# Turning attention probabilities on VectorE in 32x32 blocks, in place of identity products on TensorE

## The chip, the cores and the metric

The kernel runs on one core of a Trainium2 chip, as one launch. The metric is the time of that launch on the device in microseconds. TensorE (PE in the profile, with its weight loads as PEld) does matrix products into PSUM; VectorE (DVE), ScalarE (ACT) and GpSimd (POOL) work on the other data; SyncE (SP) issues nearly all DMA transfers. Each engine works through its own instructions in the order in which they stand; semaphores make it wait for the others.

## What is computed

A two-layer encoder trunk on 256 tokens of width 1024, in float32. Cut to what bears on the change:

```python
for layer in range(2):
    xn = rmsnorm(h)
    u, q, k, v, g_pool, g_attn = split(xn @ w_in)        # 12 heads of 128: 3 groups of 4
    pool_out = (centred means of u, minus u) @ w_pool * pool_scale
    for g, (window, dilation) in enumerate(((128, 1), (512, 4), (2048, 16))):
        logits = q_g . k_g * scale + rel_bias[bucket(offset)]   # only offsets inside the window
        o_g, lse_g = softmax(logits) @ v_g, logsumexp(logits)
    attn = sum over g of softmax(lse)_g * o_g             # one softmax over all three groups' keys
    h = h + (sigmoid(g_pool) * (pool_out @ w_a) + sigmoid(g_attn) * (attn @ w_b)) @ w_o
    xn = rmsnorm(h)
    a, gval = split(xn @ w_up)
    h = h + (gelu(conv3(a) + conv_b) * gval) @ w_down
out = rmsnorm(h)
```

## The kernel before

**Number format.** Most products are made in three: each float32 matrix is split into a high part in the faster 32-bit format of TensorE (`F32R`) and a low part, what is left. ACT casts the high part and VectorE subtracts it to get the low one. For weights these are lines 177 and 178 (`wh`, `wl`). `two_sums` (lines 482 and 484) makes one projection: eight products of 128x512 with `wh`, against the high and the low part of the activations side by side, and eight of 128x256 with `wl`.

**Weights.** The class `Weights` lists every load and every piece in the order of use. Loads go to three raw buffers through SP's queue; five buffers hold split pieces, and `get` splits three pieces ahead of the one asked for, more where buffers are free. So ACT's and VectorE's work for a product is done up to five products before TensorE comes to it.

**Order.** The layers are written out in Python. A scheduler puts each engine's instructions in order, from the program's order and its own costs; the first stage alone is scheduled by hand. Two tokens share a partition: token 2m+t is row m of half t, so a head's 256 queries are two halves of 128.

**Around the attention.** After the pooling mixer, loop `m` goes over six weight blocks of queries and keys, four projections each; then eight projections make `pa` from the pooled branch. The attention is a list `steps` that `step()` takes from between projections, so that TensorE has other work while a head's softmax is made. For each head `hh` of four (it stands for one head of each group):

- `scores` (line 866): for each half `t`, products into one PSUM tile of 128 queries x 512 keys (256 of the near group and 128 of each dilated one); VectorE adds the bias (line 881) and takes the row maximum (886), ACT takes the exponential and the sum (889), VectorE scales by the reciprocal (891, 892).
- `turn` (line 897): keys must come to the partitions for the next product. TensorE multiplies eight blocks of 128x128 with an identity (904); ACT and VectorE bring them from PSUM to a high part `pth`, a low part `ptl` and a plain `pt`.
- `weigh` (line 915): six products of `F32R` parts and plain float32 products (921, 925) into one PSUM tile, which ACT and VectorE split into `at2` (930, 931).

Steps are taken at `m >= 3` behind every second projection, and behind six of the eight of `pa`.

**Bias table.** `load_bias` and `build_bias` (lines 354 to 392) make, once, a table of bias by query and key. A one-hot matrix of 33 rows picks the bucket of every offset, and row 33 holds the mask's large negative number. Five pairs of products, with a left side of 33x4 (high part, low part), one pair for each of five kinds of block, stand between projections of the pooling mixer. The result goes to DRAM (`fd`), is written there 128 times (`sk`) and read back with shifted addresses into `bt`.

Of the kernel before, what the change touches and what calls it, by code (L numbers as in the profile page):

```python
# [10 lines left out]
F32 = mybir.dt.float32  # L11
F32R = mybir.dt.float32r
# [4 lines left out]
P = 128  # L17
# [5 lines left out]
HPG = 4  # L23
NG = 3
NH = HPG * NG
# [8 lines left out]
NT = 5  # L34
# [5 lines left out]
ENTRY = 4  # L40
# [164 lines left out]
def encoder(ctx, tc, x, w_in, w_pool, pool_scale, w_a, w_b, w_o, norm1, norm2, w_up, conv_w,  # L205
            conv_b, w_down, rel_bias, norm_f, onehot, edges, out):
    nc = tc.nc
    const = ctx.enter_context(tc.tile_pool(name="const", bufs=1))
    wpool = ctx.enter_context(tc.tile_pool(name="weights", bufs=1))
    big = ctx.enter_context(tc.tile_pool(name="big", bufs=1))  # L210
    sm = ctx.enter_context(tc.tile_pool(name="small", bufs=2))
    acc = ctx.enter_context(tc.tile_pool(name="acc", bufs=4, space=bass.MemoryType.PSUM))
# [72 lines left out]
    h = const.tile([P, 2, D], F32, name="h")  # L285
# [7 lines left out]
    ident = const.tile([P, P], F32, name="ident")  # L293
# [58 lines left out]
    bt = const.tile([P, HPG, NT * P], F32, name="bt")  # L352

    def load_bias():
        oh = big.tile([33, NT * 256], F32, tag="ybig", name="onehot_sb")
        nc.sync.dma_start(out=oh, in_=onehot)
        rb = sm.tile([33, NH], F32, tag="rb", bufs=1, name="rb")
        nc.vector.memset(rb, 1.0)
        nc.sync.dma_start(out=rb[0:32, :], in_=rel_bias)
        rh = sm.tile([33, NH], F32R, tag="ms", name="rh")  # L360
        rl = sm.tile([33, NH], F32R, tag="ms", name="rl")
        nc.vector.tensor_copy(rh, rb)
        nc.vector.tensor_sub(out=rl, in0=rb, in1=rh.bitcast(F32))
        ohr = big.tile([33, NT * 256], F32R, tag="m2", name="onehot_r")
        nc.scalar.copy(out=ohr, in_=oh)
        return rh, rl, ohr

    def build_bias(rh, rl, ohr):

        fsb = big.tile([HPG, NT * 256], F32, tag="q1", name="fsb")  # L370
        for n, g in enumerate((0, 0, 0, 1, 2)):
            ps = acc.tile([P, 512], F32, tag="acc", name="f_ps")
            for j, r in enumerate((rh, rl)):
                nc.tensor.matmul(
                    ps[:HPG, :256], r[:, g * HPG : (g + 1) * HPG], ohr[:, n * 256 : (n + 1) * 256],
                    start=(j == 0), stop=(j == 1),
                )
            nc.vector.tensor_copy(fsb[:, n * 256 : (n + 1) * 256], ps[:HPG, :256])
            yield

        n = HPG * NT * 256
        fd = dram.tile([1, n], F32, name="fd")
        nc.sync.dma_start(out=fd[0].rearrange("(h e) -> h e", h=HPG), in_=fsb)
# [190 lines left out]
    def v_sum(ps, x2, t, n, piece):  # L574
# [3 lines left out]
        for m, (part, w, j) in enumerate(passes):  # L578
# [2 lines left out]
                stop=(n == 3 and m == 5),  # L581
            )

    def two_parts(tag, name):


        return big.tile([P, KD, 2, 2, P], F32R, tag=tag, name=name)

    def begin_values_of_x():
# [24 lines left out]

        def square(t, n):
            cc = HALVES[n]
            junk = sm.tile([P, 512], F32, tag="p", bufs=3, name="junk")
            if n == 0:
                nc.scalar.activation(
                    junk, h[:, t, cc], AF.Square, scale=D**-0.5, accum_out=ss[t][:, n : n + 1]  # L620
                )
            else:
                nc.vector.scalar_tensor_tensor(
                    out=junk, in0=h[:, t, cc], scalar=1.0 / D, in1=h[:, t, cc],
                    op0=ALU.mult, op1=ALU.mult, accum_out=ss[t][:, n : n + 1],
                )
            if n == 0:
                nc.gpsimd.tensor_scalar_add(ss[t][:, 3:4], ss[t][:, 0:1], EPS)
            else:
                nc.gpsimd.tensor_add(out=ss[t][:, 3:4], in0=ss[t][:, 3:4], in1=ss[t][:, 1:2])  # L630
                return nc.gpsimd.tensor_tensor(out=rs[t], in0=ss[t][:, 3:4], in1=mhalf, op=ALU.pow)
# [8 lines left out]
        ps = [v_tile() for _ in range(2)]  # L640
# [108 lines left out]
    for l in range(DEPTH):  # L749
# [49 lines left out]
        for gi in range(3, -1, -1):  # L799
# [8 lines left out]
            cur, n = u, S + 2 * PAD  # L808
# [11 lines left out]
            e = edge[:, gi, 0:hw].unsqueeze(1).to_broadcast([P, 2, hw])  # L820
# [43 lines left out]
        probs, ptiles = {}, {}  # L864

        def scores(hh):
            for t in range(2):
                ps = acc.tile([P, 512], F32, tag="acc", name="s_ps")
                for m, (a, b) in enumerate(((qh, kh), (qh, kl), (ql, kh))):
                    nc.tensor.matmul(  # L870
                        ps[:, 0:256], a[:, hh, t, :], b[:, hh].rearrange("p t m -> p (t m)"),
                        start=(m == 0), stop=(m == 2),
                    )
# [7 lines left out]
                nc.vector.tensor_add(  # L881
                    out=s.rearrange("p (a b) -> p a b", a=2), in0=ps.rearrange("p (a b) -> p a b", a=2),
                    in1=bias_of(t, hh),
                )
                nm = sm.tile([P, 1], F32, tag="nm", name="nm")
                nc.vector.tensor_reduce(out=nm, in_=s, axis=AX.X, op=ALU.max, negate=True)
# [8 lines left out]
                probs[hh, t] = p  # L895

        def turn(hh):
            pth = sm.tile([P, 2, 2, P], F32R, tag="pth", bufs=1, name="pth")
            ptl = sm.tile([P, 2, 2, P], F32R, tag="us", name="ptl")
            pt = sm.tile([P, 2, 2, P], F32, tag="pt", bufs=1, name="pt")  # L900
            for t in range(2):
                ps = acc.tile([P, 4, P], F32, tag="acc", name="pt_ps")
                for b in range(4):
                    nc.tensor.transpose(ps[:, b, :], probs[hh, t][:, b * P : (b + 1) * P], ident)  # L904
                nc.scalar.copy(out=pth[:, :, t, :], in_=ps[:, 0:2, :])
                if t == 0:
                    nc.scalar.copy(out=pt[:, :, t, :], in_=ps[:, 2:4, :])
                else:
                    nc.vector.tensor_copy(pt[:, :, t, :], ps[:, 2:4, :])
                nc.vector.tensor_sub(  # L910
                    out=ptl[:, :, t, :], in0=ps[:, 0:2, :], in1=pth[:, :, t, :].bitcast(F32)
                )
            ptiles[hh] = pth, ptl, pt

        def weigh(hh):
            pth, ptl, pt = ptiles[hh]
# [14 lines left out]
            nc.vector.tensor_sub(out=ol, in0=ps, in1=oh.bitcast(F32))  # L931

        steps = []
        for pair in ((0, 1), (2, 3)):
            a, b = pair
            steps += [(scores, a), (turn, a), (scores, b), (weigh, a), (turn, b), (weigh, b)]

        def step():
            if steps:
                f, hh = steps.pop(0)  # L940
                f(hh)


        for m, c in enumerate(PAIRS):
# [7 lines left out]
            for n in range(4):  # L952
# [16 lines left out]
                else:  # L969
# [14 lines left out]


# [62 lines left out]

        a_first = big.tile([P, ENTRY, S], F32, tag="gates", name="a_first")

        def keep_entry(ps):
            r = sm.tile([P, ENTRY * P], F32, tag="p", bufs=3, name="a_rows")
            nc.scalar.copy(out=r, in_=ps)
            return r

# [5 lines left out]
            nc.vector.tensor_copy(av, pt)  # L1061

        held, ps = entry
        first = keep_entry(ps)
        ps = v_tile()
        for n in range(4):
            v_sum(ps, x2, 1, n, held[n])
# [1 line left out]
                turn_entry(0, first)  # L1069
        for i, _ in held:  # L1070
            W.free(i)
        last = keep_entry(ps)
        g_first = [proj(x2)]
        turn_entry(1, last)

# [96 lines left out]
```

## Time and profile before

| | |
|---|---|
| three runs | 881.98, 882.49, 882.96 us; median 882.49 us |
| profiled execution | span 880.5 us, from its first instruction to its last; its own time is not listed apart from that |
| granted TensorE clock | 0.998 of full speed |
| attention of layer 0 | about 112 to 178 us of the span |
| attention of layer 1 | about 543 to 610 us |
| bias products | 43.9 to 55.9 us |

How to read a row of instructions in order of time: start, length, engine, line, operation, what it writes and reads, shape; in brackets how long the engine had been idle and what ended that. Instructions that follow one another overlap, so the spacing of two starts says what one costs its engine, and its length says how long a reader of its result waits. In a row of groups the number after the bar is the summed time, then the mean length of one in ns, then the idle time ahead of them and what ended it.

### The profile page before, as it was taken

What the parts mean: (1) busy time and instruction counts of PE and PEld (TensorE: products, weight loads), DVE (VectorE), ACT (ScalarE), POOL (GpSimd) and SP (SyncE); (2) the same over time, 40 slices, a digit from 0 to 9 for tenths busy, and PEclk for the clock granted to TensorE, in tenths of its full rate; (3) what the DMA queues carried; (4) which work ended last, traced back from release to release, by engine and by line L of the source; (5) the groups of instructions that cost most, each with busy time, mean ns of one, the idle gap of its engine ahead of it and who ended that gap; (6) DMA issues with size and microseconds to landing.
All of it is one profiled execution on the core that took longest, in us unless ns stands there. A gap on an engine that the chain in (4) does not pass through costs nothing.

```text
span 880.5 us, 12819 instructions
## 1 busy us (share of the span) xinstructions
PE 872.5 (99%) x4849; PEld 759.1 (86%) x4849; DVE 676.9 (77%) x1151; ACT 520.3 (59%) x913; POOL 13.8 (2%) x40
## 2 busy tenths in 40 slices
PE   9999999999999999999999999999999999999996
PEld 7889889988888888888888898999888888888885
DVE  6987786767869987787756977776678698878774
ACT  7745654556648766666545564554566486666652
POOL 2000000000000000000000000000000000000000
PEclk9999999999999999999999999999999999999999
DMA  9669744455564665465736565443556447466541
GB/s 329 232 206 296 254 145 147 141 182 176 176 206 148 206 223 191 159 220 196 239 120 223 160 198 185 148 163 123 190 190 202 163 144 260 165 198 203 173 144 48
DMA packets 125789, 164.46 MB, mean 187 GB/s; under 512 B 2995, under 2 KB 106107, under 8 KB 125600
## 3 DMA queue, kind: packets, MB, share of 16 engines
q1 hardware_dynamic: 125712, 163.65, 56.0%
q8 instruction: 38, 0.62, 0.3%
q14 instruction: 23, 0.19, 0.1%
q10 hardware_dynamic: 16, 0.00, 0.0%
HBM read 162.57 MB, written 3.69 MB: 189 GB/s over the span
## 4 chain that ended last, share of the span: by engine, by line
PE 99%; ACT 0%; POOL 0%; DVE 0%; issue 0%; POOLq 0%; ACTq 0%
PE proj_ps L482 40%; PE proj_ps L484 21%; PE res_ps L510 6%; PE res_ps L509 6%; PE v_ps L579 6%; PE res_ps L511 6%; PE v_ps L741 2%; PE b_ps L482 2%; PE v_ps L654 1%; PE b_ps L484 1%; PE s_ps L875 1%; PE o_ps L925 1%; PE pt_ps L904 1%; PE s_ps L870 1%; PE o_ps L921 1%; PE xt_ps L450 1%
## 5 line engine op out<-in xcount | busy, mean ns | idle before, releaser
L178 DVE TENSOR_TENSOR wl<-raw,wh 128x1024 fp32r<-128x1024 f32 x274 | 334.1, 1222 | 137.8 <-ACT wh L177 135.4
L177 ACT CAST wh<-raw 128x1024 fp32r<-128x1024 f32 x274 | 286.1, 1049 | 194.7 <-PE proj_ps L482 134.4
L482 PE MATMUL proj_ps<-x,wh 128*128 128x512 f32 x1408 | 354.1, 393 | 0.0
L482 PEld LDWEIGHTS proj_ps<-x,wh 128*128 128x128 f32 x1408 | 254.1, 189 | 47.4 <-issue 0.5
L484 PEld LDWEIGHTS proj_ps<-x,wl 128*128 128x128 f32 x1408 | 192.0, 190 | 13.8
L484 PE MATMUL proj_ps<-x,wl 128*128 128x256 f32 x1408 | 196.3, 282 | 0.0
L509 PE MATMUL res_ps<-wh,actq 128*128 128x512 f32 (+1 forms) x184 | 70.2, 381 | 0.0
L510 PE MATMUL res_ps<-wl,actq 128*128 128x512 f32 (+1 forms) x184 | 70.1, 381 | 0.0
L511 PE MATMUL res_ps<-wh,actk 128*128 128x512 f32 (+1 forms) x184 | 69.9, 380 | 0.0
L511 PEld LDWEIGHTS res_ps<-wh,actk 128*128 128x128 f32 x184 | 34.6, 188 | 6.7
L509 PEld LDWEIGHTS res_ps<-wh,actq 128*128 128x128 f32 x184 | 34.7, 188 | 6.2
L510 PEld LDWEIGHTS res_ps<-wl,actq 128*128 128x128 f32 x184 | 34.7, 188 | 6.0
L482 PE MATMUL proj_ps<-po,wh 128*128 128x512 f32 x128 | 33.1, 400 | 0.0
L1102 ACT ACTIVATE y<-y 128x256 f32<-128x256 f32 x44 | 18.3, 416 | 24.6 <-DVE y L1099 24.6
L1085 ACT ACTIVATE y<-a,prm 128x256 f32<-128x256 f32 x36 | 21.6, 600 | 15.9 <-DVE a L505 15.9
L416 ACT ACTIVATE junk<-h 128x512 f32<-128x512 f32 (+1 forms) x20 | 10.9, 547 | 27.8 <-DVE h L414 27.8
L509 PE MATMUL res_ps<-wh,m 128*128 128x512 f32 (+1 forms) x72 | 26.5, 368 | 0.0
L482 PEld LDWEIGHTS proj_ps<-po,wh 128*128 128x128 f32 x128 | 22.9, 189 | 4.1
L510 PE MATMUL res_ps<-wl,m 128*128 128x512 f32 (+1 forms) x72 | 26.3, 366 | 0.0
L511 PE MATMUL res_ps<-wh,m 128*128 128x512 f32 (+1 forms) x72 | 26.3, 365 | 0.0
L579 PE MATMUL v_ps<-wh,x 128*128 128x512 f32 x80 | 25.7, 392 | 0.0
L1086 DVE SCALAR_TENSOR_TENSOR y<-a,prm,y 128x255 f32<-128x255 f32 x36 | 17.2, 479 | 8.1 <-ACT y L1085 8.1
(208 smaller groups left out, 1106.3 us busy)
## 6 DMA issues: line engine op xcount, KB each, us to landing
raw<-in_w_in_dram SPq DMA_DIRECT2D x58, 1024.0 KB, 5.1
raw<-in_w_up_dram SPq DMA_DIRECT2D x44, 1024.0 KB, 4.9
raw<-in_w_down_dram SPq DMA_DIRECT2D x22, 1024.0 KB, 4.8
raw<-in_w_a_dram SPq DMA_DIRECT2D x8, 1024.0 KB, 4.9
raw<-in_w_o_dram SPq DMA_DIRECT2D x8, 1024.0 KB, 4.8
raw<-in_w_b_dram SPq DMA_DIRECT2D x4, 1024.0 KB
sk<-fd SPq DMA_DIRECT2D x1, 2560.0 KB
raw<-in_w_pool_dram SPq DMA_DIRECT2D x2, 1024.0 KB
```

Of the source, the lines that this page charges most:

```text
L177: lambda: nc.scalar.copy(out=h, in_=src),
L178: lambda: nc.vector.tensor_sub(out=l, in0=src, in1=h.bitcast(F32)),
L482: nc.tensor.matmul(ps, wh(k), x2[:, k], start=(k == 0), stop=False)
L484: nc.tensor.matmul(ps[:, 1], wl(k), x2[:, k, 0], start=False, stop=(k == nk - 1))
L509: nc.tensor.matmul(ps, ah, wh, start=first, stop=False)
L510: nc.tensor.matmul(ps, ah, wl, start=False, stop=False)
L511: nc.tensor.matmul(ps, al, wh, start=False, stop=last)
L579: nc.tensor.matmul(ps, x2[:, 2 * n + j, part, t, :], w[:, j, :], start=(n + m == 0), stop=(n == 3 and m == 5),)
L741: nc.tensor.matmul(ps[t], a[:, k, t, :], w[:, j, :], start=(k + m == 0), stop=(k == KD - 1 and m == 2),)
L1085: nc.scalar.activation(y, a, AF.Identity, bias=b, scale=w1)
L1086: nc.vector.scalar_tensor_tensor(out=y[:, 1:], in0=a[:, : S - 1], scalar=w0, in1=y[:, 1:], op0=ALU.mult, op1=ALU.add)
L1102: nc.scalar.activation(y2, y2, AF.Tanh, scale=c)
```

## The change

*Turn.* The identity products and their copies out of PSUM go. VectorE's `transpose` turns blocks of 32x32 inside one group of 32 lanes and may write to another group. One instruction reads 32 lanes (32 queries of both halves) at one 32-column offset in each of four key blocks, and writes 32 lanes x 256 elements. Sixteen of them turn a head, four for each group of lanes that is read; each writes to another group than the one before. The probabilities of both halves lie in one tile `probs`, made in place from the scores. When all sixteen are done, ACT casts the high part of the first two key blocks (128x512) and VectorE subtracts it; the other two are used as they are.

*Steps.* The scores of both heads of a pair come first, and a turn is two steps of eight instructions. Eight steps go between the query and key projections of `m >= 3`, eight behind the projections of `pa`.

*Bias.* High and low part of the bucket biases stand in one 128x128 left side (rows 0 to 32 and 64 to 96, with the one-hot matrix repeated), one group's columns at each of three lane groups, zeros elsewhere. Three products of 128 rows, two 512 columns wide and one 256, replace the ten. POOL fills both tiles with zeros first, the one-hot matrix is loaded twice, the bucket biases by six small loads, and `fd` is written by three.

*Buffers.* `junk`, `probs` and `rb` use tag `s`; `a_rows` in the second sub-layer takes the buffer `m2`.

```diff
     def load_bias():
-        oh = big.tile([33, NT * 256], F32, tag="ybig", name="onehot_sb")
-        nc.sync.dma_start(out=oh, in_=onehot)
-        rb = sm.tile([33, NH], F32, tag="rb", bufs=1, name="rb")
-        nc.vector.memset(rb, 1.0)
-        nc.sync.dma_start(out=rb[0:32, :], in_=rel_bias)
...
+        oh = big.tile([P, NT * 256], F32, tag="ybig", name="onehot_sb")
+        nc.gpsimd.memset(oh, 0.0)
+        rb = sm.tile([P, P], F32, tag="s", name="rb")
+        nc.gpsimd.memset(rb, 0.0)
+        for r in (0, 64):
+            nc.sync.dma_start(out=oh[r : r + 33, :], in_=onehot)
+            for g in range(NG):
+                cc = slice(32 * g, 32 * g + HPG)
+                nc.sync.dma_start(out=rb[r : r + 32, cc], in_=rel_bias[:, g * HPG : (g + 1) * HPG])
+        for g in range(NG):
+            nc.gpsimd.memset(rb[32:33, 32 * g : 32 * g + HPG], 1.0)
+        rr = big.tile([P, P], F32R, tag="at2", name="rr")
+        nc.vector.tensor_copy(rr, rb)
+        nc.vector.tensor_sub(out=rr[64:96], in0=rb[64:96], in1=rr[64:96].bitcast(F32))
...
     def build_bias(rr, ohr):
+        fsb = big.tile([96, NT * 256], F32, tag="q1", name="fsb")
+        for c0, groups in ((0, (0, 0)), (512, (0, 1)), (1024, (2,))):
+            width = 256 * len(groups)
             ps = acc.tile([P, 512], F32, tag="acc", name="f_ps")
-            for j, r in enumerate((rh, rl)):
-                nc.tensor.matmul(
-                    ps[:HPG, :256], r[:, g * HPG : (g + 1) * HPG], ohr[:, n * 256 : (n + 1) * 256],
-                    start=(j == 0), stop=(j == 1),
-                )
+            nc.tensor.matmul(ps[:, :width], rr, ohr[:, c0 : c0 + width], start=True, stop=True)
...
+    def blocks(out, in_, quarters):
+        for i in quarters:
+            for j in range(4):
+                a, b = slice(32 * i, 32 * i + 32), slice(32 * j, 32 * j + 32)
+                nc.vector.transpose(out=out[b, :, :, a], in_=in_[a, :, :, b])
...
         def scores(hh):
+            probs[hh] = sm.tile([P, 2, 512], F32, tag="s", name="probs")
...
-                s = sm.tile([P, 512], F32, tag="s", name="s")
+                s = probs[hh][:, t]
...
-                p = sm.tile([P, 512], F32, tag="p", bufs=3, name="p")
+                p = s
...
-        def turn(hh):
...
-            for t in range(2):
-                ps = acc.tile([P, 4, P], F32, tag="acc", name="pt_ps")
-                for b in range(4):
-                    nc.tensor.transpose(ps[:, b, :], probs[hh, t][:, b * P : (b + 1) * P], ident)
-                nc.scalar.copy(out=pth[:, :, t, :], in_=ps[:, 0:2, :])
...
+        def turn(hh, n):
+            if n == 0:
+                ptiles[hh] = sm.tile([P, 4, 2, P], F32, tag="pt", bufs=1, name="pt")
+            pt = ptiles[hh]
+            blocks(
+                pt.rearrange("p c t q -> p t c q"), probs[hh].rearrange("p t (c k) -> p t c k", c=4),
+                range(2 * n, 2 * n + 2),
+            )
+            if n:
+                pth = sm.tile([P, 2, 2, P], F32R, tag="us", name="pth")
+                ptl = sm.tile([P, 2, 2, P], F32R, tag="us", name="ptl")
+                nc.scalar.copy(out=pth, in_=pt[:, 0:2])
+                nc.vector.tensor_sub(out=ptl, in0=pt[:, 0:2], in1=pth.bitcast(F32))
+                ptiles[hh] = pth, ptl, pt[:, 2:4]
...
-        for pair in ((0, 1), (2, 3)):
-            a, b = pair
-            steps += [(scores, a), (turn, a), (scores, b), (weigh, a), (turn, b), (weigh, b)]
+        for a, b in ((0, 1), (2, 3)):
+            steps += [(scores, a), (scores, b), (turn, a, 0), (turn, a, 1), (weigh, a)]
+            steps += [(turn, b, 0), (turn, b, 1), (weigh, b)]
...
-                if m >= 3 and n % 2:
+                if m >= 3 and n and len(steps) > 8:
                     step()
...
             add_up(pa[:, c, :], proj(po2))
-            if c not in (1, 6):
-                step()
+            step()
```

More of the change, by code (lines that the diff above doesn't have):

```diff
@@ new lines, in load_bias, with build_bias @@
+        rr = big.tile([P, P], F32R, tag="at2", name="rr")
+        nc.vector.tensor_copy(rr, rb)
+        nc.vector.tensor_sub(
+            out=rr[64:96], in0=rb[64:96], in1=rr[64:96].bitcast(F32)
+        )
+        ohr = big.tile([P, NT * 256], F32R, tag="m2", name="onehot_r")
+        nc.scalar.copy(out=ohr, in_=oh)
+        return rr, ohr
+    def build_bias(rr, ohr):
+        fsb = big.tile([96, NT * 256], F32, tag="q1", name="fsb")
+        for c0, groups in ((0, (0, 0)), (512, (0, 1)), (1024, (2,))):
+            width = 256 * len(groups)
+            ps = acc.tile([P, 512], F32, tag="acc", name="f_ps")
+            nc.tensor.matmul(ps[:, :width], rr, ohr[:, c0 : c0 + width], start=True, stop=True)
+            for j, g in enumerate(groups):
+                cc = slice(j * 256, (j + 1) * 256)
+                rows = slice(32 * g, 32 * g + HPG)
+                nc.vector.tensor_copy(fsb[rows, c0 + j * 256 : c0 + (j + 1) * 256], ps[rows, cc])
@@ L616, in square @@
             cc = HALVES[n]
-            junk = sm.tile([P, 512], F32, tag="p", bufs=3, name="junk")
+            junk = sm.tile([P, 512], F32, tag="s", name="junk")
             if n == 0:
@@ L894, in scores @@
                 )
-                probs[hh, t] = p
-        def turn(hh):
-            pth = sm.tile([P, 2, 2, P], F32R, tag="pth", bufs=1, name="pth")
-            ptl = sm.tile([P, 2, 2, P], F32R, tag="us", name="ptl")
-            pt = sm.tile([P, 2, 2, P], F32, tag="pt", bufs=1, name="pt")
-            for t in range(2):
-                ps = acc.tile([P, 4, P], F32, tag="acc", name="pt_ps")
-                for b in range(4):
-                    nc.tensor.transpose(ps[:, b, :], probs[hh, t][:, b * P : (b + 1) * P], ident)
-                nc.scalar.copy(out=pth[:, :, t, :], in_=ps[:, 0:2, :])
[L906 to L913, printed above, removed]
+        def turn(hh, n):
[5 more added lines that the diff above has]
+                range(2 * n, 2 * n + 2),
+            )
+            if n:
[4 more added lines that the diff above has]
+                ptiles[hh] = pth, ptl, pt[:, 2:4]
         def weigh(hh):
@@ L1049, in encoder, with keep_entry @@
         a_first = big.tile([P, ENTRY, S], F32, tag="gates", name="a_first")
-        def keep_entry(ps):
-            r = sm.tile([P, ENTRY * P], F32, tag="p", bufs=3, name="a_rows")
+        rows_of_a = big.tile([P, 2, ENTRY * P], F32, tag="m2", name="a_rows")
+        def keep_entry(t, ps):
+            r = rows_of_a[:, t]
             nc.scalar.copy(out=r, in_=ps)
@@ L1063, in encoder @@
         held, ps = entry
-        first = keep_entry(ps)
+        first = keep_entry(0, ps)
         ps = v_tile()
@@ L1071, in encoder @@
             W.free(i)
-        last = keep_entry(ps)
+        last = keep_entry(1, ps)
         g_first = [proj(x2)]
```

18 lines of the change are left out of this document (5 added, 13 removed).

## The prediction

> **What bounds the kernel now.** First the page: where the busy time is, and the chain that ended last.
>
> ```profile
> span 880.5 us, 12819 instructions
> PE 872.5 (99%) x4849; PEld 759.1 (86%) x4849; DVE 676.9 (77%) x1151; ACT 520.3 (59%) x913; POOL 13.8 (2%) x40
> ...
> PE 99%; ACT 0%; POOL 0%; DVE 0%; issue 0%; POOLq 0%; ACTq 0%
> ```
>
> TensorE is busy 99% of the span and is 99% of the chain. So a TensorE instruction taken away is worth its whole time, as long as nothing else makes TensorE wait; and any new wait of TensorE is paid in full. The profiled execution's own time is not listed beside its span; the span is 2.0 us under the median of the three runs (882.49), and I carry differences over to that median.
>
> Next the waits, those of the load queue, and then VectorE (DVE) in the stretches of layer 0 that hold the attention.
>
> ```profile
> DVE wl L178 <- ACT wh L177: 135.4, 147, 6.5
> ACT wh L177 <- PE proj_ps L482: 134.4, 107, 3.1
> ```
>
> ```profile
> SPq L117 <- DVE wl L178: 197.7, 41, 9.0
> ```
>
> ```profile
> 111.00:123.00 12.00, 12.00 (x81) 10.93 (x80) 10.62 (x22) 7.11 (x14) 0.00 (x0) 1.00 0.54 175
> 123.00:134.00 11.00, 11.00 (x73) 9.99 (x72) 8.82 (x15) 5.96 (x12) 0.00 (x0) 1.00 0.41 122
> 134.00:148.00 14.00, 14.00 (x92) 12.63 (x91) 8.00 (x13) 6.63 (x12) 0.00 (x0) 1.00 0.48 156
> 148.00:163.00 15.00, 15.00 (x100) 13.63 (x99) 10.72 (x21) 7.99 (x16) 0.00 (x0) 1.00 0.47 158
> 163.00:178.00 15.00, 15.00 (x100) 13.62 (x99) 10.72 (x21) 7.89 (x16) 0.00 (x0) 1.00 0.34 113
> ```
>
> The loads wait for DVE to free a raw buffer, DVE waits for ScalarE (ACT), ACT waits for TensorE to free one of the five weight slots: the weights run ahead of TensorE by up to five products. In the last fence the columns after the length are PE, PEld, DVE and ACT busy: in 67 us DVE is busy 48.9 (73%). A change that gives DVE more work has a quarter of this stretch, not more, and the lead of the weights.
>
> **What TensorE loses.** One turn of a head, and the products before and after it:
>
> ```profile
> 118.29 1.11 PE L484 MATMUL proj_ps<-x,wl 128*128 128x256 f32 x8
> ...
> 119.24 1.03 PE L904 MATMUL pt_ps<-ident,p 128*128 128x128 f32 x8
> ...
> 120.03 2.10 PE L482 MATMUL proj_ps<-x,wh 128*128 128x512 f32 x8
> ...
> 121.97 1.11 PE L484 MATMUL proj_ps<-x,wl 128*128 128x256 f32 x8
> ...
> 122.92 2.00 PE L482 MATMUL proj_ps<-x,wh 128*128 128x512 f32 x8
> ...
> 124.76 1.11 PE L484 MATMUL proj_ps<-x,wl 128*128 128x256 f32 x8
> ```
>
> From start to start the eight identity products take 119.24 to 120.03 = 0.79. The eight wide products behind them take 1.94, the next eight 1.84: 0.10 more for following the turn. A whole projection is 1.84 + 0.95 (121.97 to 122.92) = 2.79. Scores and weighing keep their own 0.10. Eight heads in two layers: 8 x 0.89 = 7.1 us.
>
> ```profile
> 45.62 0.28 PE L374 MATMUL f_ps<-onehot_r,rh 33*4 33x256 f32 x1
> ...
> 45.95 2.11 PE L482 MATMUL proj_ps<-x,wh 128*128 128x512 f32 x8
> ...
> 47.90 1.11 PE L484 MATMUL proj_ps<-x,wl 128*128 128x256 f32 x8
> ...
> 48.94 0.28 PE L374 MATMUL f_ps<-onehot_r,rh 33*4 33x256 f32 x1
> ```
>
> A pair of small bias products takes 0.33 itself, and the projection behind it 2.99 instead of 2.79: 0.53 a pair, 2.6 for five. The three full-size ones cost what a projection's cost from start to start, 1.84/8 = 0.23, 0.23 and half of it, 0.58 together. Gain 2.0 us. The sum on TensorE is **9.1 us**.
>
> **Edits that I cost at nothing.** The bias products move into the third of the mixer's projections.
>
> ```profile
> 42.04 0.33 PE L348 MATMUL prm_ps<-ident,prow 96*128 96x96 f32 x2
> 38.03 0.33 SPq L359 DMA_DIRECT2D rb<-in_rel_bias_dram  x1
> ```
>
> TensorE reaches them at 42.1 + 2 x 2.79 + 2.3 = 50.0 us. Their left side `rb` now takes the buffer of a parameter tile that TensorE turns at 42.0; then come a fill by POOL, six small loads in a row on SP's queue (0.33 each to issue), and two DVE operations that stand behind a weight split. I put the chain's end between 47 and 51 us (an estimate: 44.2 for the last issue, the rest landing and DVE's queue), so 0 to 1 us of wait; I take 0. The weight load queued behind the six was waiting for DVE anyway (197.7 us of such waits), as were those behind the second load of the one-hot table. The table itself is used 50 us after it is made. Scratch tiles moved to other buffers (`junk`, `a_rows`) find them free: the first squares end before the third starts, and m2's last reader is a product that is over.
>
> **What DVE gains.** A head now has 16 block turns, each on 32 lanes x 256 elements, one low-part subtraction of 128x512 in place of two of 128x256, and one copy less. No row shows a block turn. The nearest are these:
>
> ```profile
> 121.70 0.41 DVE L910 TENSOR_TENSOR ptl<-pt_ps,pth 128x256 fp32r<-128x256 f32 x1
> ...
> 122.03 0.41 DVE L909 COPY pt<-pt_ps 128x256 f32<-128x256 f32 x1
> ...
> 115.37 0.68 DVE L881 TENSOR_TENSOR s<-s_ps,bt 128x512 f32<-128x512 f32 x1
> ...
> 116.08 0.69 DVE L886 TENSOR_REDUCE nm<-s 128x1 f32<-128x512 f32 x1
> ```
>
> ```profile
> L1018 DVE TENSOR_TENSOR m<-m,m 128x256 fp32r<-128x256 f32 x16 | 6.4, 418 | 0.0
> L728 ACT CAST x<-xu 128x512 fp32r<-128x512 f32 x4 | 2.4, 614 | 1.6 <-DVE xu L723 1.6
> ```
>
> Two neighbours of 256 elements that have nothing to do with each other start 0.33 apart though each lasts 0.41: the next starts 0.08 before the last ends. Where the second must have the first's result it starts 0.03 after the end (115.37 + 0.68 = 116.05, then 116.08). So one turn, call its price T, costs **0.33** if turns overlap like the first pair and 0.42 + 0.03 = **0.45** if each waits for the last. I take 0.45, because every turn writes to another group of lanes than the one before it, and the overlap of 0.08 is shown here only for instructions that keep to the same lanes. The upper end is 0.60, the spacing of 128x512 operations, should turning take two passes.
>
> [...]
>
> **Who waits.** In the new order of TensorE each head's weighing is threaded into a projection, and it needs all 16 turns, then ACT's copy of the high part, then DVE's subtraction. Between one head's weighing and the next, TensorE has a fixed amount to do, DVE a fixed queue in order:
>
> ```profile
> 112.04 0.28 PE L870 MATMUL s_ps<-kh,qh 128*128 128x256 f32 x1
> ...
> 113.57 2.09 PE L482 MATMUL proj_ps<-x,wh 128*128 128x512 f32 x8
> ...
> 132.91 0.28 PE L921 MATMUL o_ps<-pth,vh 128*128 128x256 f32 x1
> ...
> 134.43 2.09 PE L482 MATMUL proj_ps<-x,wh 128*128 128x512 f32 x8
> ...
> 134.72 0.37 ACT L930 CAST at<-o_ps 128x256 fp32r<-128x256 f32 x1 [1.22 <-PE o_ps L925]
> 36.76 2.36 DVE L178 TENSOR_TENSOR wl<-raw,wh 128x1024 fp32r<-128x1024 f32 x2
> ```
>
> Scores and weighing are 1.53 and 1.52 on TensorE; a weight split is 2.36 - 1.22 = 1.14 on DVE, a 256-element operation 0.33, a 512-element one 0.60; ACT's copy of 128x512 is 0.61, with 0.06 (an estimate) for each of two handovers 0.73.
>
> - *Second head of a pair, first half.* Count from DVE's start on the low part of the head before. TensorE: 0.74 until it has that (0.68 + 0.06), 1.40 of weighing left, 1.51 of its projection (two wide products, 0.10, the 0.95), two whole ones (5.58), then 2.44 of the next (1.84 and five of the narrow): 11.67. DVE: low part 0.60, three splits 3.42, four small ones 1.32, 16 turns, ACT's copy 0.73: 6.07 + 16T. TensorE waits 16T - 5.6.
> - *Second head, second half.* After the same 2.14, the first turn must wait for the end of the weighing (0.29, as from 134.43 to 134.72), because `pt` has one buffer. DVE: 2.43 + two small ones, one split, 16 turns, copy = 4.96 + 16T. TensorE: 2.14 + 1.28 (one wide, 0.10, 0.95) + 5.58 + 1.61 (seven wide) = 10.61. Wait 16T - 5.65.
> - *First heads.* From the first scores, by the same prices through both scores, softmax, splits and turns, the low part is ready at 15.9 + 16T and TensorE wants it at 21.7; in the second half, 13.5 + 16T against 19.1. Wait 16T - 5.8 and 16T - 5.6.
>
> Per layer 64T - 22.65, in both 128T - 45.3. With T = 0.45: 57.6 - 45.3 = 12.3 us. The instruction after each run of eight turns also loses its 0.08 of overlap, two a head in eight heads: 1.3. **Sum: 12.3 + 1.3 - 9.1 = +4.5 us**, 882.5 + 4.5 = **887.0**. The weights do not stop TensorE: in the 67-us stretch DVE now has 48.9 - 12 x 0.33 + 4 x 0.60 + 64 x 0.45 = 76 us of work, TensorE with its waits takes 67 - 3.6 + 6.2 = 70, and the excess of 6 comes off a lead of five products (14 us).
>
> **Rivals.**
> - *The turns overlap after all* (T = 0.33 to 0.36). For it: every pair of independent neighbours in the trace overlaps. Against it: none of them changes lanes. Then 128T - 45.3 is below or about 0, the spare time in each bullet covers the turns, and the whole 9.1 stays, less 0 to 1.5: 874.0. It decides at T = 0.354 where waiting starts; break-even is at (45.3 + 9.1)/128 = 0.425, or 0.415 with the lost overlap.
> - *A turn takes as long as a 512-element operation* (T = 0.60). For it: data goes in by rows and out by columns, which nothing here does. 128 x 0.60 - 45.3 - 9.1 = +22: 905.
> - *Turns of 0.42 with no gap*: 53.8 - 45.3 + 1.3 - 9.1 = +0.7, no difference that can be measured; this measurement tells about 0.2%, 1.8 us, from no change.
>
> **How the numbers follow.** My forecast (T 0.43 to 0.48, 884 to 891) has a chance of 0.55, overlap 0.30, the gapless case 0.07, the slow turn 0.08. The range reaches down to the overlap at 874 and up to T = 0.52 (128 x 0.52 - 45.3 + 1.3 - 9.1 = +13.5), 896; the likeliest case's own range is 883 to 893. The waits are sums of some twenty rows each and may be off by 0.5 a head, 4 us in all, so a part of the forecast's chance falls to "same" and a little to "faster": faster 0.33, same 0.10, slower 0.57.
>
> **What would show it.** Right: TensorE busy about 9 us less; no L904; the new transpose on DVE at 0.42 to 0.45 each, starts as far apart as they last; TensorE waiting at the first or second product of each weighing, 1 to 2 us a head, 128 turns in all. Wrong: starts 0.33 apart and a TensorE that never waits in the attention (then 874), or a wait at the bias products, or TensorE waiting for weights in a projection, which my sum leaves out.

## The result and the profile after

| | before | after |
|---|---|---|
| median | 882.48 us (881.98 to 882.96) | 889.65 us (888.63 to 891.3) |
| span of the profiled execution | 880.5 us | 887.9 us |
| ratio of the times, with its 95% interval | | 1.0087 (1.0075 to 1.0099) |
| granted TensorE clock | 0.998 | 0.998 |

The change made the kernel 7.2 us slower. The forecast was 4.5 us slower, in the range 874 to 896. In the document below, "before" and "after" are these two kernels; the profiled execution's own time of after is 889.68 us, 1.8 us over its span.

The page of after, first its busy times, then the chain that ended last by engine and by line:

```profile
span 887.9 us, 12747 instructions
...
PE 868.2 (98%) x4778; PEld 751.5 (85%) x4778; DVE 727.5 (82%) x1262; ACT 518.8 (58%) x897; POOL 15.2 (2%) x45
...
PE 82%; DVE 13%; ACT 2%; DMA 1%; issue 1%; POOLq 0%; POOL 0%; ACTq 0%; DVEq 0%; SPq 0%
PE proj_ps L491 30%; PE proj_ps L493 16%; PE res_ps L518 6%; PE res_ps L519 6%; PE v_ps L588 6%; PE res_ps L520 6%; DVE pt L598 6%; DVE wl L178 3%; PE v_ps L757 2%; PE b_ps L491 2%; PE v_ps L670 1%; DMA raw<-in_w_in_dram 1%; PE b_ps L493 1%; PE o_ps L935 1%; PE o_ps L939 1%
```

In before the chain was TensorE at 99%. Now VectorE has 13% of it, 6% with the block turns of line 598 alone. TensorE is busy 4.3 us less in a span 7.4 us longer; VectorE is busy 50.6 us more. The groups and the waits, in which a wait's three numbers are its total in us, how often, and the longest:

```profile
L598 DVE STREAM_TRANSPOSE pt<-probs 32x256 f32<-32x256 f32 x128 | 55.7, 435 | 1.9
```

```profile
PEld o_ps L935 <- ACT pth L925: 12.2, 8, 1.9
PE o_ps L935 <- ACT pth L925: 9.2, 8, 1.5
PEld o_ps L935 <- DVE ptl L926: 4.2, 8, 1.1
...
PE o_ps L935 <- DVE ptl L926: 1.4, 2, 0.7
...
PEld f_ps L381 <- DVE rr L368: 0.2, 1, 0.2
```

All eight weighings wait for the high part `pth`, and then again for the low part `ptl`, by the rows of PEld. In order of time, the block turns and the weighings of the first two heads:

```profile
129.27 3.59 DVE L598 STREAM_TRANSPOSE pt<-probs 32x256 f32<-32x256 f32 x8
...
132.89 1.23 DVE L178 TENSOR_TENSOR wl<-raw,wh 128x1024 fp32r<-128x1024 f32 x1
132.89 0.62 ACT L925 CAST pth<-pt 128x512 fp32r<-128x512 f32 x1 [0.41 <-DVE pt L598]
...
133.57 0.39 PE L935 MATMUL o_ps<-pth,vh 128*128 128x256 f32 x1 [0.28 <-ACT pth L925]
...
134.37 0.68 DVE L926 TENSOR_TENSOR ptl<-pt,pth 128x512 fp32r<-128x512 f32 x1
...
135.11 0.38 PE L935 MATMUL o_ps<-ptl,vh 128*128 128x256 f32 x1 [0.69 <-DVE ptl L926]
...
143.41 3.59 DVE L598 STREAM_TRANSPOSE pt<-probs 32x256 f32<-32x256 f32 x8
...
147.03 0.62 ACT L925 CAST pth<-pt 128x512 fp32r<-128x512 f32 x1 [2.73 <-DVE pt L598]
...
147.70 0.38 PE L935 MATMUL o_ps<-pth,vh 128*128 128x256 f32 x1 [1.43 <-ACT pth L925]
```

Eight turns take 3.59 us and one takes 0.435, so from start to start they are (3.59 - 0.435) / 7 = 0.451 apart: the price T of the prediction. The chain is the one that it named: turns, cast, product. The low part comes later than its own work asks for: a weight split (132.89 to 134.12) and a small operation stand ahead of the subtraction in VectorE's order, so it starts at 134.37, 0.86 us after the cast has ended. Another order there was not tried. VectorE has next to no room left in that stretch; in this row the first number after the length is PE's busy time, then PEld's, DVE's and ACT's:

```profile
111.00:178.00 67.00, 63.08 (x388) 55.21 (x387) 64.70 (x129) 32.35 (x58) 0.00 (x0) 1.00 0.39 126
```

DVE is busy 64.7 of 67 us, where it was 48.9.

To see where the 7 us lie I take marks that are the same product in both kernels: the turn of the parameter tiles, the first scores of a layer, and the first product with `w_b` behind the attention. Before, then after:

```profile
42.04 0.33 PE L348 MATMUL prm_ps<-ident,prow 96*128 96x96 f32 x2
...
212.27 1.09 PE L482 MATMUL b_ps<-at,wh 128*128 128x512 f32 x4
...
543.67 0.28 PE L870 MATMUL s_ps<-kh,qh 128*128 128x256 f32 x1
...
643.89 1.09 PE L482 MATMUL b_ps<-at,wh 128*128 128x512 f32 x4
```

```profile
42.13 0.33 PE L348 MATMUL prm_ps<-ident,prow 96*128 96x96 f32 x2
...
112.20 0.28 PE L887 MATMUL s_ps<-kh,qh 128*128 128x256 f32 x1
...
216.26 1.09 PE L491 MATMUL b_ps<-at,wh 128*128 128x512 f32 x4
...
547.64 0.28 PE L887 MATMUL s_ps<-kh,qh 128*128 128x256 f32 x1
...
651.68 1.09 PE L491 MATMUL b_ps<-at,wh 128*128 128x512 f32 x4
```

| stretch | before | after | difference |
|---|---|---|---|
| parameter tiles to first scores (bias products, pooling) | 70.00 | 70.07 | +0.07 |
| first scores to `w_b`, layer 0 | 100.23 | 104.06 | +3.83 |
| first scores to `w_b`, layer 1 | 100.22 | 104.04 | +3.82 |
| last mark to the end of the span | 236.61 | 236.22 | -0.39 |

(The first scores of before start at 112.04, in a row of the prediction.) Each attention stage costs 3.8 us. A stage without any wait would take 100.23 less four turns of 0.89, 96.67 (an estimate with the prediction's price of a turn); so the waits cost 7.4 us a layer. And the bias part, which was to gain 2.0, has gained nothing at the first scores.

### The profile page after: what moved, and what is told of

Same layout as the page of the kernel before. It is cut to its first block, busy times and chain, and to the rows that moved or that the text cites. A ratio compares the mean times of both kernels' runs of the same rounds, so it can differ in the third digit from the quotient of the medians.

```text
span 887.9 us, 12747 instructions
## 1 busy us (share of the span) xinstructions
PE 868.2 (98%) x4778; PEld 751.5 (85%) x4778; DVE 727.5 (82%) x1262; ACT 518.8 (58%) x897; POOL 15.2 (2%) x45
## 4 chain that ended last, share of the span: by engine, by line
PE 82%; DVE 13%; ACT 2%; DMA 1%; issue 1%; POOLq 0%; POOL 0%; ACTq 0%; DVEq 0%; SPq 0%
PE proj_ps L491 30%; PE proj_ps L493 16%; PE res_ps L518 6%; PE res_ps L519 6%; PE v_ps L588 6%; PE res_ps L520 6%; DVE pt L598 6%; DVE wl L178 3%; PE v_ps L757 2%; PE b_ps L491 2%; PE v_ps L670 1%; DMA raw<-in_w_in_dram 1%; PE b_ps L493 1%; PE o_ps L935 1%; PE o_ps L939 1%
## 5 line engine op out<-in xcount | busy, mean ns | idle before, releaser
L598 DVE STREAM_TRANSPOSE pt<-probs 32x256 f32<-32x256 f32 x128 | 55.7, 435 | 1.9
```

The costliest lines, as they stand in the source:

```text
L598: nc.vector.transpose(out=out[b, :, :, a], in_=in_[a, :, :, b])
```

## The experiments

Two theories stood at the start. **A:** a block turn costs 0.45 because it changes the lane group, VectorE is then full, and the attention pays for it; the bias products do save their 2 us, and a late weight load takes it back. **B:** turning itself costs 0.45, or the attention waits for something else; and the bias part gains as forecast, so that the turn alone loses 9.

### The two parts by themselves

`turn_only`: after, with the old bias code.

```diff
-        rr = big.tile([P, P], F32R, tag="at2", name="rr")
+        rh = sm.tile([33, NH], F32R, tag="ms", name="rh")
+        rl = sm.tile([33, NH], F32R, tag="ms", name="rl")
...
```

> The turn of after with the bias code of before (five pairs of small products). Theory A: the three full-size bias products gain nothing, since what they save on TensorE is given back at the pooling products, which wait there for a weight load; then this kernel takes after's time less 0.2, about 889.5 us (889.0 to 890.2), 7 us over before, all of it in the two attention stages (3.5 to 4 us each). Theory B: the bias part does gain the 2.0 us of the forecast, and the turn loses 9: about 891.6 us.

890.66 us (890.03 to 891.04) beside 882.07 for before; ratio 1.0100 (1.0084 to 1.0115), 8.6 us. That lies between the two theories. Between the marks the attention stages took 104.00 and 103.99 us, as in after.

`bias_only`: before, with the new bias code.

```diff
-        rh = sm.tile([33, NH], F32R, tag="ms", name="rh")
-        rl = sm.tile([33, NH], F32R, tag="ms", name="rl")
+        rr = big.tile([P, P], F32R, tag="at2", name="rr")
...
```

> The kernel before with the new bias code alone. Theory A (given back at the pooling products): 882.5 us (882.0 to 883.0), no change; TensorE is ahead of before by about 1.6 us at 60 us of the span, and by less than 0.3 at the start of the attention of layer 0. Theory B (the forecast's term): 880.5 us, and TensorE is still ahead by 2 there.

880.87 us (880.18 to 881.89, 11 runs); ratio 0.9985 (0.9976 to 0.9994), a gain of 1.2 us (0.5 to 2.1). In the profiled execution the first scores came 69.86 us behind the parameter tiles (41.68 to 111.54), 0.14 earlier than in before. So neither theory holds in its pure form: the timed executions keep about half of the 2.0 us, and at the first scores the profiled one has hardly any. Part of what is kept lies elsewhere: from the last mark to the end of the span, before and `turn_only`, with the old bias code, took 236.61 and 236.89 us, and the nine profiled executions with the new one 236.18 to 236.25. The difference comes behind TensorE's last product; its cause was not looked for. What takes the gain back is next.

### Who takes the bias gain back

The order of SP's queue in after, and what stands behind it on ACT and DVE ahead of the pooling products:

```profile
57.70 0.58 SPq L394 DMA_DIRECT2D sk<-fd  x1
...
63.43 0.41 SPq L117 DMA_DIRECT2D raw<-in_w_in_dram  x1
...
75.57 1.05 ACT L177 CAST wh<-raw 128x1024 fp32r<-128x1024 f32 x1 [3.87 <-DMA raw<-in_w_in_dram]
...
76.53 0.65 ACT L849 CAST plh<-pd 128x512 fp32r<-128x512 f32 x1
...
77.23 0.38 PE L483 MATMUL pool_ps<-plh,wh 128*128 128x256 f32 x1 [0.37 <-ACT plh L849]
...
77.80 0.68 DVE L850 TENSOR_TENSOR pll<-pd,plh 128x512 fp32r<-128x512 f32 x1
...
78.53 0.39 PE L484 MATMUL pool_ps<-pll,wh 128*128 128x256 f32 x1 [0.92 <-DVE pll L850]
```

The load issued at 63.43 is there at 75.5, 12 us later. ACT waits 3.87 us for it with a cast of weights that TensorE doesn't need yet, and the pooled activations `plh`, which TensorE does need, stand behind that cast; `pll` stands behind the matching split on DVE. In before the same load takes as long (issued at 64.46), but there the last `plh` stands ahead of the cast that waits for it:

```profile
61.14 0.59 SPq L385 DMA_DIRECT2D sk<-fd  x1
...
64.46 0.38 SPq L117 DMA_DIRECT2D raw<-in_w_in_dram  x1
...
73.47 0.66 ACT L833 CAST plh<-pd 128x512 fp32r<-128x512 f32 x1
...
77.37 2.94 ACT L177 CAST wh<-raw 128x1024 fp32r<-128x1024 f32 x3 [1.24 <-DMA raw<-in_w_in_dram]
```

The transfer that runs meanwhile is the bias table's copy `sk`. The last two numbers of this row of after are the busy share of the DMA engines and GB/s:

```profile
58.00:66.00 8.00, 8.00 (x48) 7.04 (x47) 8.00 (x16) 5.06 (x9) 0.00 (x0) 1.00 1.00 354
```

Their share is 1.00 for these 8 us, at 354 GB/s. `late_sk` puts the copy behind that load, and issues it from between the query and key projections:

```diff
...
+        for _ in range(5):
+            yield
         sk = dram.tile([P, n + 1], F32, name="sk")
-        nc.sync.dma_start(out=sk[:, 0:n], in_=fd[0].partition_broadcast(P))
+        with tc.issue_after(W.issued[13].ins):
+            nc.sync.dma_start(out=sk[:, 0:n], in_=fd[0].partition_broadcast(P))
...
+                if l + m == 0 and n == 1:
+                    run(bias)
```

> After, with the 2.6 MB copy sk put behind the next weight load on SP's queue (it stood ahead of it). Theory A: the copy fills the DMA engines and makes that load land 12 us after its issue, and this is what TensorE waits for at the pooling products; with the load first it lands in about 3 us, the 1.5 us of waits there go and the time is about 888.0 us (887.4 to 888.4). Theory B: the waits at the pooling products have another cause (DVE or ACT late by themselves): 889.6 us, no change. Theory C: the copy then holds up the load behind it in the same way: 889.6 or more, with the wait at a later product.

```profile
63.20 0.40 SPq L117 DMA_DIRECT2D raw<-in_w_in_dram  x1
...
63.76 0.58 SPq L397 DMA_DIRECT2D sk<-fd  x1
...
68.58 1.05 ACT L177 CAST wh<-raw 128x1024 fp32r<-128x1024 f32 x1 [2.64 <-DMA raw<-in_w_in_dram]
...
69.46 0.39 SPq L117 DMA_DIRECT2D raw<-in_w_in_dram  x1
...
80.12 2.00 ACT L177 CAST wh<-raw 128x1024 fp32r<-128x1024 f32 x2 [1.53 <-DMA raw<-in_w_in_dram]
```

888.64 us (887.44 to 889.0); ratio 1.0071 (1.0058 to 1.0084), against 1.0087 for after. The load ahead of the copy lands 5.4 us after its issue (63.20 to 68.58), not the 3 that I expected. TensorE has no wait at the pooling products any more, and the first scores come 68.26 us behind the parameter tiles instead of 70.07: 1.8 us, theory A. Theory C is half right: the load behind the copy now lands 10.7 us after its issue (69.46 to 80.12), but nothing that TensorE needs soon stands behind it. The medians show 1.0 of the 1.8 (1.4 by the ratios), 0.2 short of theory A's range; in the profiled execution the rest went in the attention of layer 1, 105.16 us instead of 104.04, in a stretch from 600 to 630 us with a granted clock of 0.94, where after has 1.00.

`bias_late` has the same two edits on before, with the turns on TensorE:

> Before with the new bias code and the later copy sk, turns on TensorE as before. Theory A: the forecast's gain of the bias products was right on TensorE and lost only to the copy: 1.8 to 2.0 us under before, 880.2 us, the first scores 68.3 us behind the parameter transposes instead of 70.0. Theory B: what the later copy gained with the new turn is not to be had here: 881 us as with the new bias code alone.

879.84 us (879.73 to 880.29) beside 882.21; ratio 0.9974 (0.9963 to 0.9984). First scores at 68.28 us behind the parameter tiles, 1.72 under before; 2.4 us in the medians, and 0.36 of the difference lies behind the last mark. Theory A: the saving on TensorE was there, and it was lost to the copy. The later copy alone, on before, was not run; TensorE has no wait at the pooling products of before that it could remove.

### What makes a block turn cost 0.45

`same_lanes` leaves out the move from one lane group to another: a turn writes to the lanes that it reads.

```diff
-                nc.vector.transpose(out=out[b, :, :, a], in_=in_[a, :, :, b])
+                nc.vector.transpose(out=out[a, :, :, b], in_=in_[a, :, :, b])
```

> After, with each block turn writing to the lane group that it reads (same count, same size; blocks land in the wrong lane group, so this leaves out the move across lanes). Theory A: a VectorE instruction overlaps the one before it unless the lane group of its input or output changes, and it is this that makes a turn cost 0.45; four in a row now keep their lanes, so the spacing falls to 0.33 to 0.36 (eight in 2.8 us), two runs of eight fit under two projections (5.6), the 12 us of waits at the weighing products fall under 2 and the time is 874 to 878 us. Theory B: the turning itself costs 0.45, whatever the lanes: eight in 3.6 us, 889.6 us. Theory C: the spacing falls, but VectorE's other work in the stretch holds the weighing: 882 to 887 us.

```profile
127.59 2.86 DVE L598 STREAM_TRANSPOSE pt<-probs 32x256 f32<-32x256 f32 x8
...
143.28 0.62 ACT L925 CAST pth<-pt 128x512 fp32r<-128x512 f32 x1 [1.25 <-DVE pt L598]
...
157.38 1.08 DVE L598 STREAM_TRANSPOSE pt<-probs 32x256 f32<-32x256 f32 x3
...
161.06 1.09 DVE L598 STREAM_TRANSPOSE pt<-probs 32x256 f32<-32x256 f32 x3
```

877.87 us (877.72 to 878.02); ratio 0.9953 (0.9939 to 0.9967). Eight turns took 2.86 us instead of 3.59: (2.86 - 0.43) / 7 = 0.347 on average. Each of the two rows of three turns stays in one group of lanes; with 0.42 for the last turn of each, between the 0.41 and 0.43 of single turns there (at 158.85 and 159.74), their starts are (1.08 + 1.09 - 2 x 0.42) / 4 = 0.33 apart. A run of eight changes its lanes once, half way, so one change costs about 2.43 - 7 x 0.33 = 0.12. An attention stage took 98.53 us, so 3.7 us of waits stayed where theory A had under 2. The time and the spacing are those of theory A: turning as such, at 0.33, is no dearer than the 256-element operations of the prediction's rows, 0.33 apart; each change of the lane group costs 0.12 us (0.451 - 0.33 in after too), about the overlap of 0.08 and the gap of 0.03 of those rows together.

`same_out` exchanges the loops, so that four turns in a row write the same group and each reads another.

```diff
-        for i in quarters:
-            for j in range(4):
+        for j in quarters:
+            for i in range(4):
```

> After, with the two loops over the blocks exchanged: of four block turns that follow one another all write the same lane group and each reads another one (in after they read the same and each writes another). Theory A: a change of the lane group on either side holds the next instruction until the one before has ended: eight in 3.6 us, no change, 889.6 us (888.8 to 890.4). Theory B: only the side that is written counts: eight in 2.8 us as in the run that kept its lanes, and 876 to 879 us.

```profile
129.13 3.60 DVE L598 STREAM_TRANSPOSE pt<-probs 32x256 f32<-32x256 f32 x8
```

890.0 us (889.53 to 890.52), ratio 1.0091 (1.0074 to 1.0107), eight in 3.60 us: no change, theory A. A change on the side that is read costs the same as one on the side that is written (3.60 us for eight, and 3.59 in after). A full turn visits every pair of groups once, so in this form one of the sides changes at every step.

### Whether the waits come from VectorE's being full

`spread`: the sixteen attention steps in 26 places instead of 16.

```diff
-            steps += [(scores, a), (scores, b), (turn, a, 0), (turn, a, 1), (weigh, a)]
-            steps += [(turn, b, 0), (turn, b, 1), (weigh, b)]
+            steps += [(scores, a), (scores, b), (turn, a, 0), None, (turn, a, 1), None, (weigh, a)]
+            steps += [(turn, b, 0), None, (turn, b, 1), None, None, (weigh, b)]
...
-                if m >= 3 and n and len(steps) > 8:
+                if m >= 3 and m + n > 3:
...
-        gates = big.tile([P, 4, S], F32, tag="gates", name="gates")
+        gates = big.tile([P, 4, S], F32, tag="m2", name="gates0")
...
             th = gate(c)
+            step()
...
```

> After, with the sixteen attention steps spread over 26 places instead of 16: an empty place behind each run of eight block turns, and the last places between the eight projections of the first gate loop. Every instruction is the same, and a block turn still costs 0.45. Theory A: the waits at the weighing products come from VectorE's being full in the attention stretch (64 of 66 us), so with the same work spread over some 95 us they go; TensorE keeps what the turn took from it, and the time falls by the 15 us that the waits cost, to 874 to 877 us. Theory B: the waits come from the time that one head's chain takes (turns, cast, subtraction) wherever it stands, or VectorE's work only piles up in the gate loop, and TensorE waits there: 882 to 890 us.

```profile
PEld o_ps L935 <- DVE ptl L926: 4.3, 4, 1.1
PEld o_ps L935 <- ACT pth L925: 3.3, 4, 1.0
```

```profile
550.00:600.00 50.00, 49.06 (x298) 43.29 (x297) 48.39 (x95) 26.04 (x46) 0.00 (x0) 1.00 0.44 148
600.00:630.00 30.00, 28.43 (x159) 25.02 (x159) 28.18 (x54) 14.70 (x25) 0.00 (x0) 0.94 0.37 113
630.00:650.00 20.00, 20.00 (x119) 17.68 (x118) 15.54 (x24) 11.56 (x23) 0.00 (x0) 1.00 0.77 252
```

883.11 us (881.6 to 885.04); ratio 1.0012 (1.0002 to 1.0021): 6.5 us under after, and 6 us over theory A, inside the range of theory B. Half of the waits went: the second heads, which have two empty places ahead of their weighing, wait no more, and the four first heads, which have one, still do. Layer 0's stage took 100.28 us, 3.6 over the one without waits. Layer 1's took 101.87, with a granted clock (the column after the busy times) of 0.94 for 30 us there; before has 1.00 in that stretch.

`spread_late` adds the later copy:

> The spread steps and the bias copy sk behind the next weight load, both: if the two gains are of different stages they add, and the time is 1.0 to 1.9 us under that of the spread steps alone, about 873.5 us. If the gain of the later copy was the chance of one execution, the two are the same.

881.95 us (881.49 to 883.83); ratio 1.0004 (0.9994 to 1.0013), no difference from before. It is 1.2 us under `spread` in the medians, with the first scores at 68.27 instead of 69.92: the two gains are of different stages and add. The 873.5 rested on theory A for `spread` and fell with it.

`spread2` moves the empty places: two ahead of every weighing, none between a second head's two turn steps. It has the later copy too; the edit is against `spread_late`.

```diff
-            steps += [(scores, a), (scores, b), (turn, a, 0), None, (turn, a, 1), None, (weigh, a)]
-            steps += [(turn, b, 0), None, (turn, b, 1), None, None, (weigh, b)]
+            steps += [(scores, a), (scores, b), (turn, a, 0), None, (turn, a, 1), None, None, (weigh, a)]
+            steps += [(turn, b, 0), (turn, b, 1), None, None, (weigh, b)]
```

> The spread steps and the later copy sk, with the empty places moved: two ahead of each weighing, none between the two turn steps of a second head. The stage from the first scores to the first products of w_b took 100.23 us in before, 104.05 in after and 100.28 with one empty place; without any wait it is 100.23 less the four turns, 96.7. Theory A: only the first heads' weighings still waited (their chain of 7.2 us of turns, cast and subtraction ended 1.5 us late), and two empty places cover it: 96.7 to 97.2 us a stage, 873 to 876 us in all. Theory B: the second heads, with their empty place gone, now wait instead: about 99 a stage, 878 to 880 us.

```profile
PE 864.1 (99%) x4778; PEld 752.1 (86%) x4778; DVE 726.0 (83%) x1262; ACT 517.6 (59%) x897; POOL 15.2 (2%) x45
...
PE 93%; DVE 6%; ACT 1%; issue 0%; POOLq 0%; POOL 0%; ACTq 0%
```

```profile
PEld o_ps L938 <- DVE ptl L929: 2.4, 2, 1.2
```

875.84 us (875.69 to 876.27) beside 882.21; ratio 0.9929 (0.9916 to 0.9941): 6.4 us faster than before, with the same 128 turns and the same VectorE work as after (726.0 us busy, 727.5 there). A stage takes 98.01 and 98.00 us. One weighing in each layer, the last one, still waits for its low part, so it is between the two theories, close to A in the time. Of the 6.4 us, 2.4 are to be had without moving the turn (`bias_late`: the new bias code and the later copy); the turn on VectorE is worth the other 4 once its steps have room. The new places with the old turn were not run; before has no wait of TensorE in the attention that they could remove.

VectorE's being full is not what decides. The same stretch, in after and then in `spread2`:

```profile
112.00:178.00 66.00, 62.08 (x382) 54.28 (x381) 63.98 (x127) 31.80 (x58) 0.00 (x0) 1.00 0.40 128
```

```profile
112.00:178.00 66.00, 66.00 (x408) 59.11 (x407) 64.94 (x125) 35.09 (x63) 0.00 (x0) 1.00 0.40 135
```

VectorE is busy 64.0 of 66 us in the one and 64.9 in the other, and TensorE waits in the first alone. What counts is whether a head's chain of turns, cast and subtraction ends before TensorE comes to its weighing, which is the first half of `spread`'s theory B. The other half, work of VectorE that piles up in the gate loop, is left in one place: the last weighing of a layer stands there, and it is the one that still waits.

## Why the prediction was right or wrong, point by point

- **The price of a turn, T = 0.45: right,** 0.451. Its parts were 0.435 and a gap of 0.016, not 0.42 and 0.03; that the sum agrees so closely is luck. The prediction had no row with a change of lanes, so the choice was an estimate. It was right, and so was its reason: `same_lanes` takes away only the change of lanes, and the starts go to 0.347. The two runs `same_lanes` and `same_out` show it on both sides: starts 0.347 apart on average with the lanes kept, and 0.45 with a change on either side at every step. The 512-element price of 0.60 falls, and so does the gapless 0.42: the measured 0.451 takes the gap too.
- **The rival "the turns overlap after all"** was sized at 874, with the whole 9.1 gained less 0 to 1.5. `same_lanes`, which makes it true by leaving out the move, took 877.9: its stages still lost 1.9 us each, and at the first scores it had 0.4 of the 2.0 us of the bias part.
- **TensorE's gain from the turns, 7.1 us: right as far as can be read.** `spread2` shows it coming back as its waits go: stages of 98.0 with one wait of 1.2 us left in each, against 100.23.
- **The waits at the weighings, 12.3 + 1.3 us: right in place, a term too small by 1.2.** They cost 2 x (104.05 - 96.67) = 14.8. The rows shown have 1.43 us of idle time where the bullet gave 1.6 (a second head), and 0.28 + 0.69 where it gave 1.4 (the first one); but idle time in PE's row is not all that a stop costs (below). `same_lanes` tells the same: at its 0.347 the sum has no wait left (128 x 0.347 is 44.4, less than 45.3) beyond the 1.3 of lost overlap, and its stages lost 2 x (98.53 - 96.67) = 3.7. Which of the some twenty rows in the bullets is off is not settled.
- **The bias products, -2.0: the step that failed is in "Edits that I cost at nothing", which took the new order around the loads to be free.** The price of the products was nearly right: `bias_late` has TensorE 1.72 us earlier at the first scores. I followed the loads as far as the wait for a free buffer ("was waiting for DVE anyway"). I did not follow what stands behind a late load on ACT and DVE: the changed order there puts the last pooled activations behind a cast that waits for it, and the copy `sk`, issued 3.4 us earlier (57.70 for 61.14), still slows that load to 12 us (5.4 us for the one ahead of the copy in `late_sk`). At the first scores of the profiled execution the term was +0.07; in the timed ones `bias_only` gained 1.2. By the profiled executions some 0.4 of that lies behind the last mark; the rest is not settled.
- **The small edits at nothing** (the `rb` chain, the scratch buffers) **held:** the first bias product waited 0.2 us for `rr`, of the 0 to 1 allowed.
- **The weights do not stop TensorE in a projection: right,** after's waits of PE and PEld have no row of `proj_ps`.
- **The sign "TensorE busy about 9 us less" did not come:** it was 4.3 less. The stops cost more than they show as idle time in PE's row: 14.8, by the estimate of 96.67, against 10.6 at the weighings (last section), and 1.8 against 1.3 at the pooling products (0.37 + 0.92). By these numbers 4.7 us of the stops stand in the busy time, which accounts for the gap.

The forecast of +4.5 us was 2.7 low. The two mis-sized terms between the marks, +2.1 for the bias part and +1.2 for the waits, make 3.3. Of the 0.6 that this is too much, 0.4 is the shorter end of after, behind the last mark, and the rest is in the differences between executions.

## What to carry to other kernels

Work moved off the engine that bounds the kernel is worth its time only if its result is there when that engine comes to it. Here 18 us of VectorE's spare time in the stretch (67 - 48.9) were asked for 27, and TensorE waited; the same work with ten more places to stand, and the later copy, turned a loss of 7 us into a gain of 6, with VectorE as full as in after. Look at the consumer's place in the order before the producer's price: two empty places ahead of each weighing did what a cheaper turn was wanted for. And when an edit moves a large transfer ahead in a queue, ask which loads stand behind it, and which casts that TensorE needs stand behind the casts of those loads.

## What the runs showed of the hardware that was not expected

- On VectorE, the block turns of 32 lanes x 256 elements that kept their lane groups started about 0.33 us apart (`same_lanes`), and those whose group read (`same_out`) or group written (after) changed at every step 0.45 apart: 0.12 us for each change, either side.
- TensorE's waits at the weighings cost more than the idle time in PE's row, by the estimate of 96.67 for a stage without waits. After lists 10.6 us of PE's idle time at the weighings (9.2 + 1.4) and 16.4 in PEld's rows (12.2 + 4.2), and the stages lost 14.8; in `spread2` PEld lists 2.4, and the stages lost 2 x (98.0 - 96.67) = 2.7. In `same_lanes` PE lists none at the weighings, PEld 5.4, and the stages lost 3.7. In these kernels the load queue's waits are the nearer reading.
- The granted clock fell to 0.94 for a stretch of 30 us in the attention of layer 1 in the profiled executions of `late_sk`, `spread` and `spread_late`, where that stage took 1.1 to 1.6 us longer (105.16 us in `late_sk` for 104.04 in after; 101.87 in `spread` for 100.28 in its layer 0). Before and after have 1.00 in that stretch, and `spread2` has 1.00 from 543 to 610 us. What brings it on was not tried.
